# One-core hybrid decoder layer: more chunks multiplied with seven products instead of eight, in gate|up, down and the projections around the attentions

## The chip, the core and the metric

The kernel runs on one core of one Trainium2 chip. The metric is device time of one execution in microseconds (us). A core has a matrix engine (TensorE, PE in the profile; its weight loads are PEld), a vector engine (VectorE, DVE), a scalar engine (ScalarE, ACT), GpSimd (POOL) and SyncE (SP), which here only issues transfers. The engines run side by side and wait for each other by semaphores. VectorE and ScalarE take their instructions strictly in their own order; the program's order is fixed by hand for TensorE alone, and a scheduler orders the other engines.

## The reference, cut to what matters

256 tokens, model width 2048, float32 weights. One layer: half a SwiGLU, a mixing stage of a gated spatial MLP and a windowed attention, a cross-attention over 256 memory rows, another half SwiGLU, a final norm.

```python
def swiglu(x, w_gate, w_up, w_down):                  # w_gate, w_up 2048 x 5632, w_down 5632 x 2048
    return (jax.nn.silu(x @ w_gate) * (x @ w_up)) @ w_down

h = h + 0.5 * swiglu(rmsnorm(h, g_ffn1), w1_gate, w1_up, w1_down)
z = rmsnorm(h, g_mix) @ w_in                          # columns u | v | q | k | v'
y_a = spatial_gating(z[..., :o_q], g_v, w_s, b_s)
y_b = window_attention_sinks(z[..., o_q:o_k], z[..., o_k:o_v], z[..., o_v:], sinks)
h = h + concatenate([rmsnorm(y_a, g_a_out), rmsnorm(y_b, g_b_out)]) @ w_out
h = h + cross_attention(rmsnorm(h, g_x), rmsnorm(mem, g_mem), w_xq, w_xkv, w_xo)
h = h + 0.5 * swiglu(rmsnorm(h, g_ffn2), w2_gate, w2_up, w2_down)
return rmsnorm(h, g_final)
```

## The kernel before, in words

**Precision.** Every float32 operand is split into a high part (a cast on ScalarE, `split`, L150) and a low part (a subtraction on VectorE, L151). A float32 product is three matmuls: high by high, low by high, high by low.

**Chunks and units.** A weight chunk is 256 rows by 1024 columns, loaded as four blocks of 128 x 512 (B11, B12, B21, B22; `load`, L303). The 256 tokens are two blocks of 128, so the activations of a chunk are four blocks of 128 x 128 (A11, A12, A21, A22), held as a `Pair`. A unit (class `Unit`) accumulates a row of chunks (eight in most) in PSUM banks. A chunk of kind N or C takes eight block products, 24 matmuls; a chunk of kind S takes seven (a Strassen form), 21 matmuls, but needs sums of weight blocks (t, L314 to L318, with high and low parts th and tl) and sums of activation blocks. C is the eight-product form whose banks fit those of S (its pair holds S3 and S5), so a unit that has an S has no N beside it, apart from down and the output projections, which mix N and S. The strings `KINDS`, `KINDS_M`, `HALVES_O` and `KINDS_D` give the kinds of the chunks of a unit.

**After a unit.** When the last S is multiplied, `seven_early` takes P1, Q6 and Q7 out of their banks (one copy on ScalarE, two sums on VectorE). At the unit's end `seven_late` makes the four results with five sums on VectorE (L507 to L511).

**Stages in order.** Feed-forward 1: `plain_gu_unit` (unit 0 of gate|up, all N, fed by x as it is loaded), ten `gu_unit`s (L632, kinds `KINDS`), then down: 22 row chunks in three parts, four units over the parts (0), (0, 1), (1, 2), (2), each for one half of the columns (L665). Then the projections q, k|v, v, u from n2; memory values and keys (mv0, mv1, mk0, mk1); the output projection wo; xq from n3; the cross-attention; xo; feed-forward 2; the final norm and the stores.

**Order on TensorE.** `push` loads and splits a chunk and queues its multiplication; `turn` runs the queue one chunk late. Small work (transposes, attention, norms) sits in generators in `side`, and `side_step` puts one piece of it after every sixth matmul. `held`, `alone` and `tight` keep pieces out of some chunks. `seven_unit` (L513) first runs the side work until the attentions are done.

**Buffers.** Raw weights have three buffers, their high and low parts (wh, wl) two each, t, th and tl one each. Pairs come from `fp` (14 forms), small scratch from `tmp` (tag s2). PSUM has four banks for accumulators and four (`trp`) for P1, Q6, Q7 and all small work. In `attend` one such bank (`wop`, L933) collects the results of eight heads.

Of the kernel before, what the change touches and what calls it, by code (L numbers as in the profile page):

```python
# [8 lines left out]
F32 = mybir.dt.float32  # L9
# [11 lines left out]
WARM = 12  # L21
# [11 lines left out]
def layer_kernel(  # L33
# [29 lines left out]
    tmp = ctx.enter_context(tc.tile_pool(name="tmp", bufs=7))  # L63
# [21 lines left out]
    raw0 = s2("n0r").rearrange("p (k t) -> p k t", k=2)  # L85
    nc.scalar.dma_start(raw0, xT[:T, :].rearrange("(k p) t -> p k t", p=P))
# [36 lines left out]
    last_mean = [None]  # L123

    def rstd_of(parts, n, width, nt=TB):
# [7 lines left out]
        last_mean[0] = nc.vector.tensor_scalar(ms, ss, 1.0 / width, EPS, op0=ALU.mult, op1=ALU.add)  # L133
# [19 lines left out]
    def products(o, passes):  # L153
# [8 lines left out]

    BASE = {
        "N": ("A11", "A21", "A12", "A22"),
        "C": ("A11", "A12", "A21", "A22"),
        "S": ("A21", "A11", "A22", "A12"),
    }
    SUMS = {"N": (), "C": ("S3", "S5"), "S": ("S3", "S1", "S2", "S4")}
# [5 lines left out]
    class Pair:  # L174
        def __init__(self, s, kind, base=None):
            self.kind = kind
            self.base = base or form(s)
            if kind == "S":
                self.sums = form(s)
            elif kind == "C":  # L180
# [7 lines left out]
        def __getitem__(self, name):  # L188
            names, part = BASE[self.kind], self.base
            if name not in names:  # L190
                names, part = SUMS[self.kind], self.sums
            i = names.index(name)
            return part[0][:, i, :], part[1][:, i, :]

    def fill(s, p, raw):
# [5 lines left out]
        elif p.kind == "S":  # L201
# [4 lines left out]
        if p.kind == "S":  # L206
# [39 lines left out]
    def pair_loaded(s, raw, i, gcol, base):  # L246
        p = Pair(s, "N", base)
        for k in range(2):
            c = gcol + 2 * i + k
            hi, lo = [row_tile("N", t, k) for t in p.base]  # L250
            split_scaled(hi, lo, raw[:, k, :].rearrange("p (b t) -> p b t", b=2), sm[:, c:c + 1])
        return p
# [50 lines left out]
    def load(s, w, kind, pieces):  # L303
# [5 lines left out]
        if kind == "S":  # L309
            nc.sync.dma_start(raw, w)  # L310
            t = stream.tile([P, 4, 512], F32, tag="t", name=nm(s + "t"), bufs=1)
            th = stream.tile([P, 4, 512], F32R, tag="th", name=nm(s + "th"), bufs=1)
            tl = stream.tile([P, 4, 512], F32R, tag="tl", name=nm(s + "tl"), bufs=1)
# [6 lines left out]
            split(th, tl, t)  # L320
            for i, name in enumerate(("T1", "T3", "T2", "T4")):
                b[name] = th[:, i, :], tl[:, i, :]
        elif pieces:
            for i in pieces:
# [9 lines left out]
    class Unit:  # L334


        def __init__(self, s, kinds, late=("P1", "Q6", "Q7", "R"), alone=(), sparse=False):
# [10 lines left out]
            self.begun = set()  # L348
            self.banks = {}
# [4 lines left out]
        def multiply(self, kind, p, b, by_bank):  # L354

            steps, behind = [], []
            for name, *terms in PRODUCTS[kind]:
# [3 lines left out]
                for an, bn in terms:  # L361
                    (ah, al), (bh, bl) = p[an], b[bn]
# [3 lines left out]
            for n, (name, x, y) in enumerate(steps + behind):  # L366
# [7 lines left out]
            chunks_done[self.s] = chunks_done.get(self.s, 0) + 1  # L374
# [57 lines left out]
    def push(u, i, w, p, post=None, pieces=None, beside=None):  # L432
        b = load(u.s, w, u.kinds[i], pieces)
# [3 lines left out]
        def run():  # L437
# [5 lines left out]
            u.multiply(u.kinds[i], p(), b, i in (0, len(u.kinds) - 1))  # L443
# [6 lines left out]
    def unit(s, w, cb, pairs, late, beside=None):  # L450

        u = Unit(s, "N" * 8)
# [7 lines left out]
    def narrow_unit(s, w, pairs, late, beside):  # L460

        ps = []
        for c in range(2):
# [7 lines left out]
            def run(c=c, wh=wh, wl=wl):  # L471
                if c == 0:
                    ps.extend(acc.tile([P, 512], F32, tag="acc", name=nm(s)) for _ in range(TB))
                for k in range(8):
                    p = have(pairs, (c * 8 + k) // 2)
                    side_step()
                    for tb in range(TB):
                        hi, lo = p[f"A{tb + 1}{k % 2 + 1}"]
# [8 lines left out]
    KINDS = "CCSCSCSC"  # L487
    KINDS_M = "CCSCSCSC"

# [4 lines left out]
    KINDS_D = "NNNNSNSN" + "NNSNSNN" + "NNSNSNN"  # L494
# [18 lines left out]
    def seven_unit(s, w, cb, pairs, dst, late=None):  # L513

        u = Unit(s, KINDS_M, sparse=True)
        until(lambda: len(attended) == 2 * TB)
        got = {}

        def end():
            seven_late(u, got, dst)  # L520
# [3 lines left out]
        for i in range(8):  # L524
            push(
                u, i, w[i, cb], lambda i=i: have(pairs, i),
                (lambda: seven_early(u, got)) if i == 6 else end if i == 7 else None,
            )

    def adds(s, c, j0, on_block=None):  # L530
# [33 lines left out]
        def late(u):  # L564
            for name, tb, j in BLOCKS:
                add(hb(tb, j), u[name], tb, j)
                if on_block is not None:
                    on_block(j0 + j, tb)
# [15 lines left out]
    def ffn(s, get, rs, wgu, wd, on_block, first=None):  # L584
# [35 lines left out]
        def gu_unit(c):  # L620
# [11 lines left out]
            u = Unit(s + "g", KINDS)  # L632
            for i in range(8):
                push(
                    u, i, wgu[i, c], lambda i=i: get(i),
                    lambda i=i: seven_early(u, got) if i == 6 else late(u) if i == 7 else None,
                    beside=lambda i: (
                        rs() if (c, i) == (0, 5) else inner(i - 5) if c == 10 and i >= 5 else None
# [3 lines left out]
        def plain_gu_unit(c):  # L642
            pairs_, prep, rs0 = first
# [9 lines left out]
            for i in range(8):  # L653
                push(
                    u, i, wgu[i, c], lambda i=i: have(pairs_, i), late if i == 7 else None,
                    pieces=(1, 3, 0, 2) if c + i == 0 else None, beside=prep,
# [12 lines left out]
        for n, idx in enumerate(turns):  # L669
# [4 lines left out]
            for q, i in enumerate(idx):  # L674
                at += 1

                def ahead(q, at=at, kinds=kinds):
# [3 lines left out]
                    if kinds[q] == "N" and todo:  # L681
                        inner(todo[0])

                push(
                    u, q, wd[i, half], lambda i=i: (inner(i), pairs[i])[1],
                    lambda q=q, u=u, early=early, late=late, kinds=kinds:
                        early(u) if q == kinds.rindex("S") else late(u) if q == len(kinds) - 1 else None,
                    beside=ahead,
# [78 lines left out]
    ahead = [raw0]  # L767

    def prep1(i):
        if i % 2 == 0:  # L770
# [3 lines left out]
        raw = ahead.pop()  # L774
# [3 lines left out]
        if i == 2:  # L778
            blocks_of_x(2)
        n0.append(pair_loaded("n0", raw, i, G_FFN1, [t[:, i % 2] for t in quad]))  # L780
        if i == 1:
            blocks_of_x(0)
        for j in {3: (0, 1), 4: (2, 3)}.get(i, ()):
            for tb in range(TB):
                square_into(parts1[:, tb, j:j + 1], h[:, tb, j * 512:(j + 1) * 512], 512)
        if i == 4:
# [572 lines left out]
```

## Time and profile before

| | us |
|---|---|
| median of 3 runs | 2082.5 (2082.36 to 2082.59) |
| the profiled execution | 2082.59 |
| its span, first to last instruction | 2080.9 |
| PE busy | 2065.4 (99%) |
| DVE busy | 1684.6 (81%) |
| ACT busy | 1137.1 (55%) |

An engine is busy while one of its instructions runs; instructions that overlap are counted once in the tables by stretches, and each at its own length in the groups by line. The chain of work that ended last is followed back from the last instruction, at each step to what released it. A wait is put down to the instruction that came last.

### The profile page before, as it was taken

What the parts mean: (1) busy time and instruction counts of PE and PEld (TensorE: products, weight loads), DVE (VectorE), ACT (ScalarE), POOL (GpSimd) and SP (SyncE); (2) the same over time, 40 slices, a digit from 0 to 9 for tenths busy, and PEclk for the clock granted to TensorE, in tenths of its full rate; (3) what the DMA queues carried; (4) which work ended last, traced back from release to release, by engine and by line L of the source; (5) the groups of instructions that cost most, each with busy time, mean ns of one, the idle gap of its engine ahead of it and who ended that gap; (6) DMA issues with size and microseconds to landing.
All of it is one profiled execution on the core that took longest, in us unless ns stands there. A gap on an engine that the chain in (4) does not pass through costs nothing.

```text
span 2080.9 us, 23813 instructions
## 1 busy us (share of the span) xinstructions
PE 2065.4 (99%) x9518; PEld 1712.7 (82%) x9518; DVE 1684.6 (81%) x1621; ACT 1137.1 (55%) x1104; POOL 30.2 (1%) x51
## 2 busy tenths in 40 slices
PE   9999999999999999999999999999999999999998
PEld 7788888888888888888888888888888888888886
DVE  5988888888987845968888656798888888889877
ACT  7655555555544655555555455665555555555444
POOL 0000000000000000200000000000000000000000
PEclk9999999999999999999999999999999999999999
DMA  8555555555555564535555544455555555555563
GB/s 305 182 199 206 201 191 182 207 198 195 202 201 202 198 227 167 184 137 201 189 195 186 181 160 143 181 194 210 182 206 197 203 184 202 202 202 202 185 219 121
DMA packets 60111, 402.16 MB, mean 193 GB/s; under 512 B 6864, under 2 KB 8928, under 8 KB 12768
## 3 DMA queue, kind: packets, MB, share of 16 engines
q1 hardware_dynamic: 57280, 393.50, 52.7%
q0 software_dynamic: 2016, 6.30, 0.9%
q8 instruction: 74, 1.21, 0.2%
q10 hardware_dynamic: 704, 0.84, 0.1%
q14 instruction: 37, 0.30, 0.0%
HBM read 398.52 MB, written 2.10 MB: 193 GB/s over the span
## 4 chain that ended last, share of the span: by engine, by line
PE 97%; DVE 2%; ACT 1%; issue 0%; DMA 0%; POOLq 0%; POOL 0%; SPq 0%; DVEq 0%
PE f2gQ L368 16%; PE f1gQ L368 15%; PE f2dQ L368 6%; PE f1dQ L368 6%; PE f2gP L368 6%; PE f1gP L368 5%; PE f2dP L368 3%; PE f1dP L368 3%; PE woQ L368 2%; PE xoQ L368 2%; PE xqQ L368 2%; PE f2dR L368 2%; PE f1dR L368 2%; PE mk1Q L368 1%; PE mk0Q L368 1%; PE mv1Q L368 1%
## 5 line engine op out<-in xcount | busy, mean ns | idle before, releaser
L151 DVE TENSOR_TENSOR f1gwl<-f1gw,f1gwh 128x2048 fp32r<-128x2048 f32 (+1 forms) x91 | 185.7, 2042 | 55.8 <-ACT f1gwh L150 55.6
L150 ACT CAST f2gwh<-f2gw 128x1536 fp32r<-128x1536 f32 (+1 forms) x88 | 154.3, 1753 | 133.2 <-PE f2gQ L368 97.6
L150 ACT CAST f1gwh<-f1gw 128x2048 fp32r<-128x2048 f32 (+1 forms) x91 | 155.9, 1714 | 126.0 <-PE f1gQ L368 89.4
L151 DVE TENSOR_TENSOR f2gwl<-f2gw,f2gwh 128x1536 fp32r<-128x1536 f32 (+1 forms) x88 | 183.6, 2087 | 41.1 <-ACT f2gwh L150 40.9
L368 PE MATMUL f2gQ<-f2gwh,n4fh 128*128 128x512 f32 x363 | 141.4, 390 | 0.0
L368 PE MATMUL f2gQ<-f2gwh,n4fl 128*128 128x512 f32 x363 | 141.3, 389 | 0.0
L368 PE MATMUL f1gQ<-f1gwh,n1fh 128*128 128x512 f32 x330 | 128.8, 390 | 0.0
L368 PE MATMUL f1gQ<-f1gwh,n1fl 128*128 128x512 f32 x330 | 128.5, 389 | 0.0
L150 ACT CAST f1dwh<-f1dw 128x2048 fp32r<-128x2048 f32 (+1 forms) x44 | 79.1, 1797 | 84.5 <-PE f1dQ L368 65.3
L150 ACT CAST f2dwh<-f2dw 128x2048 fp32r<-128x2048 f32 (+1 forms) x44 | 79.1, 1797 | 83.3 <-PE f2dQ L368 67.8
L368 PE MATMUL f2gQ<-f2gwl,n4fh 128*128 128x512 f32 x363 | 115.7, 392 | 0.0
L151 DVE TENSOR_TENSOR f1dwl<-f1dw,f1dwh 128x2048 fp32r<-128x2048 f32 (+1 forms) x44 | 94.2, 2143 | 26.1 <-ACT f1dwh L150 23.5
L151 DVE TENSOR_TENSOR f2dwl<-f2dw,f2dwh 128x2048 fp32r<-128x2048 f32 (+1 forms) x44 | 94.2, 2143 | 22.8 <-ACT f2dwh L150 20.0
L368 PE MATMUL f1gQ<-f1gwl,n1fh 128*128 128x512 f32 x330 | 105.1, 392 | 0.0
L151 DVE TENSOR_TENSOR f2gtl<-f2gt,f2gth 128x2048 fp32r<-128x2048 f32 x33 | 75.6, 2291 | 17.9 <-ACT f2gth L150 17.4
L151 DVE TENSOR_TENSOR f1gtl<-f1gt,f1gth 128x2048 fp32r<-128x2048 f32 x30 | 68.7, 2291 | 16.7 <-ACT f1gth L150 16.2
L368 PEld LDWEIGHTS f2gQ<-f2gwh,n4fl 128*128 128x128 f32 x363 | 68.1, 188 | 14.2
L368 PEld LDWEIGHTS f2gQ<-f2gwh,n4fh 128*128 128x128 f32 x363 | 68.2, 188 | 14.1
L368 PEld LDWEIGHTS f2gQ<-f2gwl,n4fh 128*128 128x128 f32 x363 | 67.3, 188 | 13.5
L150 ACT CAST f2gth<-f2gt 128x2048 fp32r<-128x2048 f32 x33 | 63.1, 1912 | 24.8 <-DVE f2gt L318 20.0
L368 PEld LDWEIGHTS f1gQ<-f1gwh,n1fl 128*128 128x128 f32 x330 | 62.0, 188 | 12.8
L368 PEld LDWEIGHTS f1gQ<-f1gwh,n1fh 128*128 128x128 f32 x330 | 62.0, 188 | 12.8
(700 smaller groups left out, 5714.7 us busy)
## 6 DMA issues: line engine op xcount, KB each, us to landing
f2gw<-in_w_gu SPq DMA_DIRECT2D x88, 1024.0 KB, 4.8
f1gw<-in_w_gu SPq DMA_DIRECT2D x87, 1024.0 KB, 4.8
f1dw<-in_w_down SPq DMA_DIRECT2D x44, 1024.0 KB, 4.8
f2dw<-in_w_down SPq DMA_DIRECT2D x44, 1024.0 KB, 4.8
wow<-in_w_out SPq DMA_DIRECT2D x16, 1024.0 KB, 4.8
xqw<-in_w_xq SPq DMA_DIRECT2D x16, 1024.0 KB, 4.8
xow<-in_w_xo SPq DMA_DIRECT2D x16, 1024.0 KB, 4.8
qw<-in_w_in SPq DMA_DIRECT2D x8, 1024.0 KB, 4.9
```

Source lines behind the costliest of these rows:

```text
L150: nc.scalar.copy(hi, src)
L151: nc.vector.tensor_tensor(lo, src, hi.bitcast(F32), ALU.subtract)
L368: nc.tensor.matmul(self.banks[name], x, y, start=name not in self.begun, stop=self.left[name] == 0)
```

## The change

Chunks of kind S take the place of C or N: in units 2 to 9 of each gate|up (four of eight instead of three, and the S come first, `MORE`), in down (`KINDS_D`: parts 0 and 1 get one more S each), and in q, v and both xq units (two of eight each, where there was none; n2 and n3 are made with sums for that, as n4 was). Pair 0 of n1 and n4 gets a kind D, which holds both the sums of S and those of C, since units 1 and 10 use it as C. Before, `seven_early` ran at chunk 6; it still does in every unit, now found by the last S.

The tiles th and tl are cut in two halves (T1, T3 and T2, T4), each split by itself. In `attend` the results of each group of heads are copied out of a bank of their own. The wait for the attentions at the head of `seven_unit` is gone. The start loads x by rows ahead of the first weights and moves part of the preparation of n1 into unit 1. The last two chunks of feed-forward 2 are multiplied together, token block 0 first, and each block is finished (`finished`) as soon as it is complete. `tmp` has 6 buffers instead of 7, and 8 warming matmuls stand for 12.

```diff
-WARM = 12
+WARM = 8
-    tmp = ctx.enter_context(tc.tile_pool(name="tmp", bufs=7))
+    tmp = ctx.enter_context(tc.tile_pool(name="tmp", bufs=6))
-    nc.scalar.dma_start(raw0, xT[:T, :].rearrange("(k p) t -> p k t", p=P))
...
+        if p.kind == "D":
+            d = s2(s + "d")[:, :256].rearrange("p (k t) -> p k t", k=2)
+            nc.vector.tensor_tensor(d, raw[:, 1::2, :], raw[:, 0::2, :], ALU.subtract)
+            split(p.more[0], p.more[1], d)
...
-            split(th, tl, t)
+            for i, names in enumerate((("T1", "T3"), ("T2", "T4"))):
+                th, tl = [
+                    stream.tile([P, 2, 512], F32R, tag=f"{n}{i}", name=nm(s + n), bufs=1)
+                    for n in ("th", "tl")
+                ]
+                split(th, tl, t[:, 2 * i:2 * i + 2, :])
...
+        def multiply_two(self, first, second, between):
+            steps = [self.passes("N", p, b, True)[0] for p, b in (first, second)]
+            half = len(steps[0]) // 2
+            for tb in range(TB):
+                for k in range(tb * half, (tb + 1) * half, half // 2):
+                    for s in steps:
+                        self.run(s[k:k + half // 2])
+                between(tb)
...
-    KINDS = "CCSCSCSC"
+    KINDS = "DCSCSCSC"
+    FEWER, MORE = "CCSCSCSC", "SCSCSCSC"
     KINDS_M = "CCSCSCSC"
+    KINDS_MIX = "CCCSCCSC"
+    KINDS_X = "CCCSCCSC"
-    KINDS_D = "NNNNSNSN" + "NNSNSNN" + "NNSNSNN"
+    KINDS_D = "NNSNSNSN" + "NSNSNSN" + "NNSNSNN"
...
-        until(lambda: len(attended) == 2 * TB)
...
-            u = Unit(s + "g", KINDS)
+            u = Unit(s + "g", MORE if 2 <= c <= 9 else FEWER)
...
+                if on_token_block is not None and n == 3 and q >= len(kinds) - 2:
+                    def ending(tb, u=u, late=late):
+                        with tc.high_priority():
+                            late(u, (tb,))
+                            on_token_block(tb)
...
-        for j in {5: (0,), 6: (1,), 7: (2, 3)}.get(i, ()):
+        for j in {6:(0,),8:(1,),10:(2,),12:(3,)}.get(i, ()):
             normalized(j)
...
-    unit("q", w_in, 2, n2, late_q, beside_queries)
+    seven_unit("q", KINDS_MIX, w_in, 2, n2, None, late_q, beside_queries)
...
-            po = bank("wop")
+                po = bank("wop")[:, :per * 64].rearrange("p (a d) -> p a d", a=per)
+                nc.scalar.copy(ybh[:, hs, :], po)
...
-    unit("v", w_in, 1, n2, late_v)
+    seven_unit("v", KINDS_MIX, w_in, 1, n2, None, late_v, alone=(7,))
-    unit("u", w_in, 0, n2, late_u, beside_u)
+    unit("u", w_in, 0, n2, late_u, beside_u, alone=(0,7))
...
-        unit(
-            "xq", w_xq, cb, n3, lambda ps, cb=cb: late_xq(cb, ps),
+        seven_unit(
+            "xq", KINDS_X, w_xq, cb, n3, None, lambda at, cb=cb: late_xq(cb, at),
```

## Rows read from the trace of the kernel before

**Rows 1.** The page: the busy totals, and the chain that ended last.

```profile
PE 2065.4 (99%) x9518; PEld 1712.7 (82%) x9518; DVE 1684.6 (81%) x1621; ACT 1137.1 (55%) x1104; POOL 30.2 (1%) x51
PE 97%; DVE 2%; ACT 1%; issue 0%; DMA 0%; POOLq 0%; POOL 0%; SPq 0%; DVEq 0%
```

**Rows 2.** Busy time by stretches: stretch, length, each engine, clock, DMA share, GB/s.

```profile
60.00:102.78 42.78, 42.13 (x191) 33.85 (x190) 38.94 (x43) 26.02 (x27) 0.00 (x0) 1.00 0.55 196
...
780.00:943.00 163.00, 163.00 (x807) 134.69 (x806) 115.73 (x184) 88.88 (x149) 13.85 (x19) 1.00 0.46 162
...
1165.00:1300.00 135.00, 134.10 (x694) 113.70 (x693) 82.68 (x84) 70.73 (x85) 0.69 (x1) 1.00 0.44 156
...
1836.00:2069.00 233.00, 233.00 (x1033) 193.02 (x1032) 200.98 (x191) 119.82 (x97) 0.00 (x0) 1.00 0.52 185
...
1457.85:1500.28 42.43, 42.43 (x192) 35.14 (x192) 36.36 (x31) 22.67 (x17) 0.00 (x0) 1.00 0.56 198
```

**Rows 3.** The chain in order of time: start, length, engine and matmul count.

```profile
124.81 3.40 PE f1gQ L368 x15
```

**Rows 4.** VectorE's groups by line and shape: count, busy us, mean ns, idle before.

```profile
L151 DVE TENSOR_TENSOR f2gwl<-f2gw,f2gwh 128x2048 fp32r<-128x2048 f32 x55 | 125.7, 2286 | 31.2 <-ACT f2gwh L150 31.1
L151 DVE TENSOR_TENSOR f2gtl<-f2gt,f2gth 128x2048 fp32r<-128x2048 f32 x33 | 75.6, 2291 | 17.9 <-ACT f2gth L150 17.4
...
L151 DVE TENSOR_TENSOR f2gwl<-f2gw,f2gwh 128x1536 fp32r<-128x1536 f32 x33 | 57.9, 1755 | 9.9 <-ACT f2gwh L150 9.8
...
L314 DVE TENSOR_TENSOR f2gt<-f2gw 128x1024 f32<-128x1024 f32 x33 | 40.3, 1221 | 0.6
...
L318 DVE TENSOR_TENSOR f2gt<-f2gt,f2gw 128x512 f32<-128x512 f32 x33 | 22.7, 688 | 0.7
...
L151 DVE TENSOR_TENSOR mkh<-mkT,mkh 128x1024 fp32r<-128x1024 f32 x4 | 4.9, 1220 | 0.5 <-ACT mkh L150 0.5
...
L202 DVE TENSOR_TENSOR f1af<-f1a 128x256 f32<-128x256 f32 x6 | 2.3, 417 | 0.0
```

**Rows 5.** VectorE in order of time, end of one gate|up unit: start, length, [idle before].

```profile
1484.40 2.29 DVE L151 TENSOR_TENSOR f2gtl<-f2gt,f2gth 128x2048 fp32r<-128x2048 f32 x1 [0.76 <-ACT f2gth L150]
1488.89 2.29 DVE L151 TENSOR_TENSOR f2gwl<-f2gw,f2gwh 128x2048 fp32r<-128x2048 f32 x1 [2.19 <-ACT f2gwh L150]
1492.52 2.29 DVE L151 TENSOR_TENSOR f2gwl<-f2gw,f2gwh 128x2048 fp32r<-128x2048 f32 x1 [1.33 <-ACT f2gwh L150]
1494.73 0.68 DVE L501 TENSOR_TENSOR f2gv<-f2gQ,f2gp 128x512 f32<-128x512 f32 x1
```

**Rows 6.** ScalarE's groups by line and shape: a cast of 1024 columns.

```profile
L150 ACT CAST mkh<-mkT 128x1024 fp32r<-128x1024 f32 x4 | 4.2, 1055 | 2.7 <-PE xs L155 2.7
```

**Rows 7.** TensorE's waits over the span: total us, times, longest.

```profile
PE xoP L368 <- ACT xofh L150: 0.7, 1, 0.7
PE f1gQ L368 <- DVE f1gtl L151: 0.6, 1, 0.6
```

**Rows 8.** The start in order of time, ScalarE and TensorE.

```profile
6.18 0.51 ACT L144 ACTIVATE n0h<-n0r,sm 128x256 fp32r<-128x256 f32 x1 [0.84 <-DMA n0r<-in_xT]
...
6.74 0.50 PE L368 MATMUL f1gP<-f1gwh,n0h 128*128 128x512 f32 x1 [0.41 <-ACT n0h L144]
...
9.51 0.63 PE L368 MATMUL f1gP<-f1gwl,n0h 128*128 128x512 f32 x1
...
9.94 0.63 PE L368 MATMUL f1gQ<-f1gwh,n0h 128*128 128x512 f32 x1
...
15.38 0.39 PE L368 MATMUL f1gP<-f1gwh,n0h 128*128 128x512 f32 x1
```

**Rows 9.** The end in order of time: last sum, last power, last store issued.

```profile
2070.61 0.69 DVE L537 SCALAR_TENSOR_TENSOR h<-f2dQ,h 128x512 f32<-128x512 f32 x1
...
2073.36 0.93 POOL L135 TENSOR_TENSOR rs<-ms,mhalf 128x1 f32<-128x1 f32 x1 [0.92 <-DVE ms L133]
...
2075.53 0.48 SPq L1283 DMA_DIRECT2D out<-hg  x1
```

More of the change, by code (lines that the diff above doesn't have):

```diff
@@ L177, in __init__ @@
             self.base = base or form(s)
-            if kind == "S":
+            if kind in "SD":
                 self.sums = form(s)
+                if kind == "D":
+                    self.more = [
+                        const.tile([P, 2, P], F32R, tag="more" + t, name=nm(s + "more")) for t in "hl"
+                    ]
             elif kind == "C":
@@ L191, in __getitem__ @@
                 names, part = SUMS[self.kind], self.sums
+                if kind == "C" and self.kind == "D":
+                    names, part = SUMS["C"], self.more
             i = names.index(name)
@@ L301, in layer_kernel, with load @@
     }
-    def load(s, w, kind, pieces):
+    def load(s, w, kind, pieces, between):
         raw = stream.tile([P, 4, 512], F32, tag="raw", name=nm(s + "w"), bufs=3)
@@ L365, in multiply, with run @@
                     last.append((name, ah, bl))
-            for n, (name, x, y) in enumerate(steps + behind):
+            return steps, behind
+        def run(self, steps):
+            for n, (name, x, y) in enumerate(steps):
                 self.left[name] -= 1
@@ L430, in turn, with push @@
         later[:] = [(n - 1, f) for n, f in later if n]
-    def push(u, i, w, p, post=None, pieces=None, beside=None):
-        b = load(u.s, w, u.kinds[i], pieces)
+    def push(u, i, w, p, post=None, pieces=None, beside=None, before=None, ending=None):
+        if before is not None and i:
+            before(i)
+        b = load(u.s, w, u.kinds[i], pieces, lambda n: before(i, n) if i == 0 else None)
         if beside is not None:
@@ L448, in layer_kernel, with unit @@
     BLOCKS = (("P2", 0, 0), ("Q3", 0, 1), ("R", 1, 1), ("Q4", 1, 0))
-    def unit(s, w, cb, pairs, late, beside=None):
-        u = Unit(s, "N" * 8)
+    def unit(s, w, cb, pairs, late, beside=None, alone=()):
+        u = Unit(s, "N" * 8, alone=alone)
         for i in range(8):
@@ L526, in seven_unit @@
                 u, i, w[i, cb], lambda i=i: have(pairs, i),
-                (lambda: seven_early(u, got)) if i == 6 else end if i == 7 else None,
+                lambda i=i: (i == kinds.rindex("S") and seven_early(u, got), i == 7 and end()),
+                beside=beside,
             )
@@ L635, in gu_unit @@
                     u, i, wgu[i, c], lambda i=i: get(i),
-                    lambda i=i: seven_early(u, got) if i == 6 else late(u) if i == 7 else None,
+                    lambda i=i: (
+                        i == u.kinds.rindex("S") and seven_early(u, got), i == 7 and late(u)
+                    ),
                     beside=lambda i: (
-                        rs() if (c, i) == (0, 5) else inner(i - 5) if c == 10 and i >= 5 else None
+                        first[2](8 + i) if first is not None and c == 1
+                        else rs() if (c, i) == (0, 5) else inner(i - 5) if c == 10 and i >= 5 else None
                     ),
@@ L642, in plain_gu_unit @@
         def plain_gu_unit(c):
-            pairs_, prep, rs0 = first
+            pairs_, before, prep, rs0 = first
             u = Unit(s + "g", "N" * 8, alone=(7,))
@@ L766, in layer_kernel, with first_pairs @@
     quad = []
-    ahead = [raw0]
-    def prep1(i):
-        if i % 2 == 0:
+    ahead = []
+    def first_pairs(i, piece=None):
+        if i % 2 == 0 and not piece:
             quad[:] = [
@@ L773, in prep1 @@
             ]
-        raw = ahead.pop()
+        if not piece:
+            n0.append(Pair("n0", "N", [t[:, i % 2] for t in quad]))
+            if piece is not None:
+                ahead.append(s2("n0r").rearrange("p (k t) -> p k t", k=2))
+        for k in range(2) if piece is None else (piece,) if piece < 2 else ():
+            if piece is not None:
+                nc.sync.dma_start(ahead[0][:, k, :], xT[k * P:(k + 1) * P, :])
+            row_loaded(n0[i], ahead[0], i, k, G_FFN1)
+        if piece in (None, 1):
+            ahead.pop()
+    def prep1(i):
         if i < 7:
@@ L1254, in layer_kernel @@
     hg = [[m4("hg") for _ in range(2)] for _ in range(TB)]
+    known = [tiny.tile([P, 1], F32, tag="known", name=nm("known")) for _ in range(TB)]
+    summed = [[] for _ in range(TB)]
     def on_final(j, tb):
-        square_into(partsf[tb][:, j:j + 1], h[:, tb, j * 512:(j + 1) * 512], 512)
+        part = partsf[tb][:, j:j + 1]
+        square_into(part, h[:, tb, j * 512:(j + 1) * 512], 512)
+        summed[tb].append(part)
+        if len(summed[tb]) == 2:
+            nc.vector.tensor_tensor(known[tb], *summed[tb], ALU.add)
+        elif len(summed[tb]) == 3:
+            nc.vector.tensor_tensor(known[tb], known[tb], part, ALU.add)
+            nc.vector.tensor_scalar(known[tb], known[tb], 1.0 / D, EPS, op0=ALU.mult, op1=ALU.add)
         if j < 2:
```

177 lines of the change are left out of this document (94 added, 83 removed).

## Prediction, made before the changed kernel was run

> **What bounds the kernel now.** I read the page's totals first. TensorE is busy for 99% of the span and the chain that ended last is 97% TensorE [rows 1]; VectorE, at 81%, is the only other engine near its end. Then the table by stretches [rows 2]: in a steady gate|up unit (the last row of the group, 1457.85 to 1500.28) TensorE is busy for all of 42.43 us, VectorE for 36.36, ScalarE for 22.67, and the transfers take 0.56 of the DMA engines. So a unit lasts as long as its matmuls. One matmul of 512 columns costs 0.2267 us, 3.40/15 [rows 3]; a unit of five eight-product chunks (24 matmuls) and three seven-product chunks (21) has 183 of them, 41.5 us, and the remaining 0.9 us are its transposes. A removed matmul therefore gives 0.2267 us as long as VectorE keeps up, and what VectorE has left is 42.43 - 36.36 = 6.1 us per unit. That is the question of the whole change: it takes matmuls from TensorE and pays with VectorE work.
>
> **Matmuls removed.** Each chunk that turns from eight products to seven loses 3. Gate|up: one more in each of units 2 to 9, in two feed-forwards, 16 chunks, 48 matmuls, 10.9 us. Down: `KINDS_D` gains one S in part 0 and one in part 1, each used twice, in two feed-forwards, 8 chunks, 24 matmuls, 5.4 us. q, v and the two xq units get two S each, 24 matmuls, 5.4 us. Sum: 96 matmuls, 21.8 us, if nothing else moves.
>
> **What VectorE pays in gate|up.** An eight-product chunk costs it one subtraction of 2.286 us; a seven-product chunk costs the sums t (1.221 + 0.688 + 0.688, L317 being like L318), the low part of 1536 columns (1.755) and that of t (2.291), 6.64 us in all [rows 4]. One chunk converted: +4.35 us. All four low parts of t are also cut in halves, and two of 1024 columns take 2 x 1.220 against 2.291 [rows 4], +0.15 each, 0.6 per unit. So a changed unit asks VectorE for 36.36 + 4.35 + 0.6 = 41.3 us, and TensorE for 42.43 - 0.68 = 41.75. Instructions that wait for nothing start some 0.08 us before the end of the one ahead (1492.52 + 2.29 = 94.81, and the next starts at 94.73 [rows 5]), so the real demand is nearer 41.0. VectorE keeps 0.4 to 0.8 us of idleness in a unit instead of 6.1.
>
> The halves deserve a word, since the same rows price them both ways: a cut costs 0.15 us of VectorE and lets the low part start after a cast of 1.055 [rows 6] instead of one of twice that width, in a place where VectorE stood 0.76 us for that cast (1484.40 [rows 5]). The Trainium skill (VectorE: DVE Perf Modes, The TRN2 errata) speaks against it: a fixed cost is paid by each instruction whatever its width, so one large tile pays once and halves pay twice. The rows agree (2.44 against 2.29); by the page's formula of 151 cycles over the width the cut costs about 0.16 us, an estimate, and the unit would be the same 41.3.
>
> Can VectorE be that full without TensorE waiting? The waits it has now come in the second half of a unit: 0.76, 2.19 and 1.33 us for ScalarE's casts [rows 5], which themselves wait for TensorE to give the weight buffers back. That is running ahead, not being late; the new work goes into that room. The hard place is the border of two units. A unit now begins with an S, in order by bank, so its low parts are due within 0.5 to 4 us of the border, and in the same stretch VectorE owes two sums (`seven_early`), five (`seven_late`), and the S itself, 2.6 + 1.76 + 2.44: 1.4 + 3.4 + 6.8 = 11.6 us, less 0.7 of overlapped starts, 10.9. From the last plain chunk's due time (5.0 before the border) to the last due time (3.9 after it) there are 8.9 us. So VectorE must reach that place some 2 us early, with t already summed. In the six chunks before it gains: a pair S+C costs 8.9 against 10.2 of matmuls, 1.3 us each. By hand the order just fits, with handovers to ScalarE in between that I can't place. Ends: no stall (0), and a unit that is no shorter than now plus 0.5 (1.2 us per unit, 19 us). I take 0.3 per unit, 16 x 0.3 = **4.8 us** given back, nearer to none since TensorE lost nothing in these units so far: its largest waits in the whole trace after the start are 0.6 and 0.7 us [rows 7].
>
> **Down.** The second down stage: 233.0 us, VectorE 201.0 [rows 2]. Added: 4 x 4.35, 16 cuts x 0.15, and two more pairs with sums, each at most three subtractions of 0.417 and one more low part as wide as L318, 0.69 [rows 4], 3.9 for both: 23.7, so 224.7 of 230.3. That is 98%, and in the first unit of the stage (three S of eight, the pairs still being made, the last gate|up unit's sums pending) I count 44 us of VectorE against 41.5 of matmuls. Cover is what it ran ahead. Ends 0 and 4 per stage; I take 1, **2 us** for both.
>
> **Around the attentions.** Conversions 8 x 4.5, four units' seven sums (4 x 4.8), and the pairs of n2 and n3 with sums (about 12): some 67 us of VectorE, most of it in stretches where it idles 47 of 163 and 52 of 135 us [rows 2]. It fits, cost 0. In `attend` twelve small evictions replace a bank held for eight heads; ScalarE is busy 89 of 163 there, cost 0, and 2 if a score's eviction queues behind them. After xq the rows pass VectorE (`seven_late`) before ScalarE scales them, about 0.7 us later than now, and TensorE already waits 0.7 us for the end of that chain, in xo [rows 7]: ends 0 and 2, I take **0.7**.
>
> **First two units.** x now comes in two row loads, the first ahead of the weights on SP's queue. Today the first scaled row waits for its load until 6.18, the first matmul is at 6.74, and the second chunk starts at 15.38, 8.6 us for 24 matmuls worth 5.4; the pace near 9.5 is 0.43 us, the 1.2 GHz level [rows 8]. Half the bytes, queued first instead of behind `sm`, should bring the row about when the first weight piece comes, some 1 us earlier; the weights are queued one issue (0.4 us) later. I take **-1.0**, ends -2.5 and +1.5 (four fewer warming matmuls leave TensorE idle before the first row). Against it, three quarters of the pairs n1 move from unit 0 into unit 1: 6 pairs of 1.5 to 2.4 us, 11.6 us, onto a unit whose own VectorE work is some 35, in 44 to 45 of TensorE with the transposes; today unit 1 shows 38.9 of 42.8 [rows 2]. That is 2 us over, partly covered by unit 0: ends 0 and 3, I take **+1.0**. The third sum form of pair 0 (D) is 0.8 us once, inside this.
>
> **The tail.** The last sum starts at 2070.61, the last power ends at 2073.36 + 0.93, the last store is issued at 2075.53 [rows 9], and the span ends at 2080.9. In the new order token block 0 is summed, scaled and stored while block 1 multiplies (half of the last two chunks, 5.4 us). Block 1's chain is the same sum, square, mean and power, without waiting behind block 0's: about 1 us less on VectorE and POOL, and half the bytes at the end. Against it, the last two chunks now need both weights together, the second one's a chunk earlier than today, up to 1 us. I take **-1.7**, ends -3 and 0. One scratch buffer fewer (`tmp`, 7 to 6) lies under all stages; cost 0, inside the stalls taken above.
>
> **Sum:** -21.8 + 4.8 + 2 + 0.7 - 1.0 + 1.0 - 1.7 = -16.0. On the profiled execution, 2080.9 of span and 1.7 around it, 2066.6; the median of the runs is 0.1 lower: **2066.5 us**.
>
> **Rivals.** (a) VectorE becomes the bound of both feed-forwards: changed units stay near 42.4 and down wins nothing. Then 10.9 + 5.4 are lost instead of 6.8: -6.5, 2076. For: 41.0 to 41.3 of 41.75 leaves no room for waits it can't help. Against: most of its present waits are running ahead. (b) Everything is hidden: -21.8 - 2.7 + 1 = 2059. For: no stall of TensorE in any unit now. (c) Slower: at each border the S-first chunk finds VectorE at its due time, not ahead, and TensorE stands the whole 2 us worked out above; 16 x 2 = 32 in place of 4.8 gives +11, 2094. It decides from the point at which VectorE comes to the last chunk's low part less than 2 us early. Against: the 3.5 us it waits just before that place today. (d) The stalls of (a) also lower TensorE's clock. The trace shows one such fall, near 9.5, after a broken start, and that first chunk lost 3.2 us in all, 8.6 - 5.4 [rows 8]; half of it, 1.6, once per changed unit in addition to (a) is 26 us: 2102. But the wait of 0.7 us in xo [rows 7] stands in a stretch whose granted clock is 1.00 [rows 2]. The Trainium skill (TensorE: Matmul & The Clock Gate, HAM oscillation) has this as its warning, idle gaps putting the array back to half rate again and again; here only the start bears it out.
>
> **How the numbers follow.** Chances: forecast 0.50 (2061 to 2072), (a) 0.28 (2072 to 2080), (b) 0.15, (c) 0.05, (d) 0.02. The range leaves out (c), (d), the last us of (a) and the lower third of (b): 2058 to 2079. A measurement of this kernel can tell about 0.2%, 4.2 us, from no change: faster takes the forecast, (b) and three quarters of (a), 0.86; same the rest of (a), 0.07; slower (c) and (d), 0.07.
>
> **What would show it.** Changed gate|up units of 41.8 to 42.1 us with VectorE at 97% or more, and TensorE's waits there short and for a low part; that row of the second down stage near 231; first matmul before 6; the last store issued about 4 us after the last matmul. Wrong if units stay above 42.4, if the waits sit on PSUM banks at the border, or if the granted clock falls below 1.00 inside them.

## The result, and the profile after

The changed kernel takes 2063.66 us (2063.09 to 2064.23) against 2082.43 us for the one before on the same chip: a ratio of 0.991, 95% interval 0.9898 to 0.9922, so 18.8 us or 0.9% faster. The forecast was 2066.5, range 2058 to 2079. The profiled execution took 2063.49 us, its span is 2061.7 against 2080.9, and all of the following accounts for these 19.2 us.

The page of the changed kernel: busy time of each engine, and the chain that ended last.

```profile
PE 2043.0 (99%) x9414; PEld 1690.3 (82%) x9414; DVE 1845.6 (90%) x1973; ACT 1220.6 (59%) x1341; POOL 36.0 (2%) x53
PE 97%; ACT 1%; DVE 1%; issue 0%; DMA 0%; SPq 0%; POOL 0%; POOLq 0%; DVEq 0%; ACTq 0%
```

Against [rows 1] TensorE is still the bound (99%), now for 22.4 us less, while VectorE went from 81% to 90% for 161 us more work. Table by stretches of the changed kernel (stretch, length, each engine, clock, DMA share, GB/s): a changed unit of either gate|up, unit 1 of the first, and the second down stage, to set beside [rows 2].

```profile
263.76:305.56 41.80, 41.80 (x190) 34.49 (x189) 39.96 (x38) 24.08 (x21) 0.00 (x0) 1.00 0.55 202
1531.65:1573.47 41.82, 41.82 (x189) 34.49 (x189) 40.11 (x39) 24.23 (x22) 0.00 (x0) 1.00 0.55 201
52.00:96.60 44.60, 43.70 (x208) 35.82 (x207) 43.66 (x55) 33.78 (x45) 0.00 (x0) 1.00 0.48 171
1823.50:2051.00 227.50, 227.50 (x1010) 188.35 (x1009) 215.85 (x231) 126.01 (x119) 0.00 (x0) 1.00 0.52 185
```

The changed unit is 41.8 us long, not 42.43, and TensorE is busy in all of it; VectorE has 40.0 to 40.1 (96%) where the forecast had 41.0 to 41.3. The clock is 1.00 in all four stretches. TensorE's waits over the changed kernel's span (total us, times, longest), the lines of [rows 7]:

```profile
PE xoQ L400 <- ACT n4r L248: 2.5, 1, 2.5
PE f1gP L400 <- ACT f1gwh L146: 2.2, 2, 1.3
PE woQ L400 <- ACT n3r L248: 1.5, 1, 1.5
...
PE f1gQ L400 <- DVE f1sg L658: 0.9, 1, 0.9
PE qTp L928 <- ACT qs L914: 0.7, 1, 0.7
PE xoP L400 <- ACT xofh L146: 0.7, 1, 0.7
```

There is no wait for a low part of t. The two largest past the start are new and lie where nothing was expected: in xo (2.5) and in wo (1.5). The stages, each from its first matmul on the bank of its name to the next one's, us:

| stage | before | after | difference |
|---|---|---|---|
| start, unit 0 of the first gate\|up | 55.4 | 54.0 | -1.4 |
| unit 1 | 45.9 | 46.5 | +0.6 |
| units 2 to 10 | 381.9 | 376.8 | -5.1 |
| first down | 235.1 | 231.3 | -3.8 |
| q, v, u, attention | 352.9 | 352.2 | -0.7 |
| wo | 91.7 | 93.1 | +1.4 |
| xq | 103.5 | 100.7 | -2.7 |
| xo | 102.8 | 105.7 | +2.9 |
| second gate\|up | 469.1 | 463.0 | -6.1 |
| second down, to the last sum | 232.4 | 229.7 | -2.7 |
| after the last sum | 10.3 | 8.7 | -1.6 |

### The profile page after: what moved, and what is told of

The parts are those of the page before. It is cut to its first block, busy times and chain, and to the rows that moved or that the text cites. A ratio compares the mean times of both kernels' runs of the same rounds, so it can differ in the third digit from the quotient of the medians.

```text
span 2061.7 us, 24483 instructions
## 1 busy us (share of the span) xinstructions
PE 2043.0 (99%) x9414; PEld 1690.3 (82%) x9414; DVE 1845.6 (90%) x1973; ACT 1220.6 (59%) x1341; POOL 36.0 (2%) x53
## 4 chain that ended last, share of the span: by engine, by line
PE 97%; ACT 1%; DVE 1%; issue 0%; DMA 0%; SPq 0%; POOL 0%; POOLq 0%; DVEq 0%; ACTq 0%
PE f2gQ L400 16%; PE f1gQ L400 15%; PE f1dQ L400 6%; PE f2dQ L400 6%; PE f2gP L400 6%; PE f1gP L400 6%; PE xqQ L400 3%; PE f1dP L400 3%; PE f2dP L400 3%; PE woQ L400 2%; PE xoQ L400 2%; PE f1dR L400 2%; PE f2dR L400 2%; PE vQ L400 2%; PE qQ L400 2%; PE mk1Q L400 1%
## 5 line engine op out<-in xcount | busy, mean ns | idle before, releaser
L146 ACT CAST f1gwh<-f1gw 128x1536 fp32r<-128x1536 f32 (+2 forms) x94 | 152.9, 1628 | 87.3 <-PE f1gQ L400 54.7
L147 DVE TENSOR_TENSOR f1gwl<-f1gw,f1gwh 128x1536 fp32r<-128x1536 f32 (+2 forms) x94 | 181.7, 1935 | 23.9 <-ACT f1gwh L146 23.8
L147 DVE TENSOR_TENSOR f2gwl<-f2gw,f2gwh 128x1536 fp32r<-128x1536 f32 (+1 forms) x88 | 179.3, 2037 | 11.0 <-ACT f2gwh L146 10.9
L400 PE MATMUL f2gQ<-f2gwh,n4fl 128*128 128x512 f32 x317 | 123.4, 389 | 0.0
L146 ACT CAST f2gth<-f2gt 128x1024 fp32r<-128x1024 f32 x82 | 84.8, 1049 | 52.3 <-DVE f2gt L323 42.0
L146 ACT CAST f1gth<-f1gt 128x1024 fp32r<-128x1024 f32 x76 | 78.8, 1050 | 57.4 <-DVE f1gt L323 44.1
L147 DVE TENSOR_TENSOR f2gtl<-f2gt,f2gth 128x1024 fp32r<-128x1024 f32 x82 | 99.5, 1218 | 10.1 <-ACT f2gth L146 9.6
L147 DVE TENSOR_TENSOR f1gtl<-f1gt,f1gth 128x1024 fp32r<-128x1024 f32 x76 | 92.3, 1218 | 9.0 <-ACT f1gth L146 8.4
L400 PE MATMUL f2gQ<-f2gwl,n4fh 128*128 128x512 f32 x317 | 97.0, 390 | 0.0
L400 PE MATMUL f1gQ<-f1gwl,n1fh 128*128 128x512 f32 x286 | 87.1, 390 | 0.0
L400 PE MATMUL f2gP<-f2gwh,n4fh 128*128 128x512 f32 x176 | 69.5, 395 | 0.0
```

Source lines behind the costliest of these rows:

```text
L146: nc.scalar.copy(hi, src)
L147: nc.vector.tensor_tensor(lo, src, hi.bitcast(F32), ALU.subtract)
L400: nc.tensor.matmul(self.banks[name], x, y, start=name not in self.begun, stop=self.left[name] == 0)
```

## Experiments

All are edits of the changed kernel; "costs" means against its 2063.66 us, ratios are against the kernel before on the same chip, with 95% intervals. Two stretches differ between profiled executions without an edit there: the start (unit 0 ended between 52.8 and 55.0 us in the kernels that share it) and xo, where a fall of the clock adds 1.4 to 1.7 us in some (last section). So an edit is read from the stages that it touches, and the cost of the whole kernel stands beside it.

### The fourth seven-product chunk

```diff
-            u = Unit(s + "g", MORE if 2 <= c <= 9 else FEWER)
+            u = Unit(s + "g", FEWER)
```

> The changed kernel with the fourth seven-product chunk taken out of units 2 to 9 of both gate|up stages; all else stays. Theory (TensorE bounds these units and VectorE has room): 16 chunks give back 48 matmuls, about 0.63 us per unit as the two traces show (42.43 against 41.80), so 16 x 0.63 = 10 us longer, near 2073.7; VectorE in such a unit near 36.5 of 42.4. Rival (VectorE close to its bound, as forecast, 0.3 us per unit lost to it): only 6 us longer, near 2070.

Measured: 2074.92 us, ratio 0.9962 (0.995 to 0.9975). Each gate|up became 5.1 us longer (428.4, counted from unit 1, and 468.1), 0.64 us a unit: 10.2 of the 10.9 us that 48 matmuls are worth. So what the fourth chunk's VectorE work costs TensorE is about 0.05 us a unit, not the 0.3 of the forecast. (The whole kernel is 11.3 us longer; in its profiled execution 1.6 of that are the clock in xo.)

### Down with its old kinds

```diff
-    KINDS_D = "NNSNSNSN" + "NSNSNSN" + "NNSNSNN"
+    KINDS_D = "NNNNSNSN" + "NNSNSNN" + "NNSNSNN"
```

> The changed kernel with the kinds of the chunks of down as before. Theory (no stall in down): 24 matmuls of 0.2267 us return, 5.4 us longer, near 2069.1. Rival (the forecast's 1 us of stall in each down stage goes away with them): 3.4 us longer, near 2067.

Measured: 2068.38 us, ratio 0.9934 (0.9922 to 0.9947); 2.7 us more in each down stage (the first: 234.1, the second: 232.4), 5.5 in all, the whole worth of the 24 matmuls, 5.4. Nothing is given back there.

### The high and low parts of t in one piece

```diff
-            for i, names in enumerate((("T1", "T3"), ("T2", "T4"))):
...
+            th, tl = [
+                stream.tile([P, 4, 512], F32R, tag=n, name=nm(s + n), bufs=1) for n in ("th", "tl")
+            ]
+            split(th, tl, t)
+            for i, name in enumerate(("T1", "T3", "T2", "T4")):
+                b[name] = th[:, i, :], tl[:, i, :]
```

> The changed kernel with the high and low parts of t in one tile each, split whole, as before the change. Theory A (the halves are what lets a unit of four seven-product chunks run without waits: a whole tile is given back only after the last of its products, and its low part starts after a cast of 1.9 us instead of 1.05): TensorE waits for the low part of t, 0.3 to 1 us per changed unit and some in down, 5 to 20 us longer. Theory B (a fixed cost per instruction is all that the cut brings): VectorE gets 0.3 to 0.6 us per unit back, TensorE was not waiting, 0 to 1 us longer or shorter.

Measured: 2139.0 us, ratio 1.0269 (1.0255 to 1.0283): 75 us slower than with halves, and slower than the kernel before. The first gate|up took 455.8 us (+32.5), the second 490.4 (+27.4), the first down 239.0 (+7.6) and the second down 237.7 (+8.0). Units 2 to 9 are 3.6 us longer each. Theory A has the direction and the waits, but at most a quarter of the size. TensorE's waits in this kernel:

```profile
PE f1gQ L398 <- DVE f1gtl L147: 13.3, 9, 1.7
PE f2gQ L398 <- DVE f2gtl L147: 12.7, 8, 1.7
```

And VectorE in order of time (start, length, idle before), with the matmul at a unit's border and one of ScalarE's casts:

```profile
243.15 2.28 DVE L147 TENSOR_TENSOR f1gtl<-f1gt,f1gth 128x2048 fp32r<-128x2048 f32 x1
...
245.49 0.50 PE L398 MATMUL f1gQ<-f1gtl,n1fh 128*128 128x512 f32 x1 [1.65 <-DVE f1gtl L147]
...
261.75 0.69 DVE L323 TENSOR_TENSOR f1gt<-f1gt,f1gw 128x512 f32<-128x512 f32 x1
...
262.56 1.91 ACT L146 CAST f1gth<-f1gt 128x2048 fp32r<-128x2048 f32 x1 [3.87 <-DVE f1gt L323]
...
264.50 2.29 DVE L147 TENSOR_TENSOR f1gtl<-f1gt,f1gth 128x2048 fp32r<-128x2048 f32 x1 [2.06 <-ACT f1gth L146]
...
275.18 2.29 DVE L147 TENSOR_TENSOR f1gtl<-f1gt,f1gth 128x2048 fp32r<-128x2048 f32 x1 [2.05 <-ACT f1gth L146]
```

In the middle of the unit VectorE stands 2.06 us for the cast of the whole t. That cast had not waited for a buffer: ScalarE stood 3.87 us for VectorE's last sum of t (261.75 + 0.69), began 0.12 us after it and took 1.91 us, and only then could the subtraction start. The changed kernel at the same place of a unit, VectorE and ScalarE:

```profile
239.93 1.23 DVE L319 TENSOR_TENSOR f1gt<-f1gw 128x1024 f32<-128x1024 f32 x1
...
241.26 1.05 ACT L146 CAST f1gth<-f1gt 128x1024 fp32r<-128x1024 f32 x1 [0.66 <-DVE f1gt L319]
...
242.74 0.68 DVE L322 TENSOR_TENSOR f1gt<-f1gt,f1gw 128x512 f32<-128x512 f32 x1
...
244.48 0.68 DVE L323 TENSOR_TENSOR f1gt<-f1gt,f1gw 128x512 f32<-128x512 f32 x1
```

With halves the first one is cast before the last two sums of t are made, each cast is 1.05 us, and a unit has one wait of VectorE for such a cast, 1.19 us, in place of two of 2 us. (That the cast waited for TensorE to give th back, which theory A names as well, stands in the gate|up stages of this trace once: 6.7 us, in unit 2 of the first, where TensorE then lost 3.5.) The 4 us lost in each unit make VectorE late at the border, and TensorE waits 1.65 us there. This is rival (c) at the place that the prediction named, and with the smaller waits behind it at 3.6 us a unit where (c) had 2; the halves are what keeps it away. The 0.15 us that a cut costs is a tenth of what it saves at one such wait.

### A scratch buffer more, and the waits in xo and wo

```diff
-    tmp = ctx.enter_context(tc.tile_pool(name="tmp", bufs=6))
+    tmp = ctx.enter_context(tc.tile_pool(name="tmp", bufs=7))
```

(with some small tiles at one or two buffers, to make room)

> The changed kernel with 7 scratch buffers as before the change (the room comes from small statistics tiles that never had more than one or two owners). Theory (the two new waits of TensorE in wo and xo, 1.5 and 2.5 us for a bank whose transposed rows ScalarE had not yet copied out, come from the missing scratch buffer that this copy writes): both vanish, 4 us shorter, near 2059.7. Rival (they come from ScalarE's order, which has the weight casts ahead of that copy, with more work than before in the pairs): unchanged within 1 us.

Measured: 2064.93 us, ratio 0.9915 (0.9901 to 0.9928), and the same two waits, 2.5 and 1.5 us. The scratch buffer isn't their cause. What is, the changed kernel's order of time shows (ScalarE, then TensorE):

```profile
1334.10 1.47 ACT L146 CAST xowh<-xow 128x1536 fp32r<-128x1536 f32 x1
...
1335.47 1.04 ACT L146 CAST xoth<-xot 128x1024 fp32r<-128x1024 f32 x1
...
1336.42 0.83 ACT L248 ACTIVATE n4r<-n,sm 128x256 f32<-128x256 f32 x2
...
1337.30 0.50 PE L400 MATMUL xoQ<-xoth,xofh 128*128 128x512 f32 x1 [2.54 <-ACT n4r L248]
```

Rows of n4 have been transposed into a PSUM bank; the copy out of it is queued on ScalarE behind two casts of weights, 1.47 and 1.04 us, and the next matmul needs a bank. ScalarE is the fullest engine there, 95% against VectorE's 89% (the changed kernel, then the one before at about the same place):

```profile
1320.00:1337.00 17.00, 14.75 (x73) 11.90 (x71) 15.13 (x21) 16.23 (x25) 1.42 (x3) 1.00 0.71 261
```

```profile
1334.00:1351.00 17.00, 17.00 (x84) 14.11 (x83) 15.41 (x22) 15.41 (x23) 0.00 (x0) 1.00 0.63 228
```

Before, ScalarE had 15.41 us of the 17, and TensorE no wait. Around the wait in wo ScalarE has 13.35 us of 14, and had 8.64 before.

### When the pairs of the next norm are made

```diff
-            yield 4 if i % 2 == 0 and mixed else 1
+            yield (8 if i % 2 == 0 else 3) if mixed else 1
```

> The changed kernel with the pairs of n2, n3 and n4 made further apart (a pause of 8 and 3 steps in place of 4 and 1 ahead of each pair's transposes). Theory (the waits in wo, 1.5 us, and xo, 2.5 us, come from ScalarE, busy 95% of the 17 us around them with weight casts and these pairs in one queue): both waits shrink or vanish, with the fall of the granted clock that follows the longer one in some executions (1.7 us), 3 to 6 us shorter, near 2059. Rival (the work only collides with the next seven-product chunk): unchanged within 1 us, the waits at another place.

Measured: 2063.13 us, ratio 0.9908 (0.9893 to 0.9923). As the rival had it, the waits in wo and xo are gone (wo -1.8, xo -2.8 us), and the same amount came back elsewhere: xq +1.7, q +1.1, second gate|up +1.6, with new waits of 1.4 us on a weight cast of xq and 0.8 on rows of n2. For n4 alone (6 and 2 in place of 4 and 1):

> The changed kernel with the pairs of n4 alone made further apart (pauses of 6 and 2 steps in place of 4 and 1). Theory (in the run that did so for n2, n3 and n4 the xo stage gained 2.8 us, but the next stages lost as much, since later pairs met other casts; half the delay keeps the gain): the wait of 2.5 us in xo and the fall of the clock behind it go, and unit 0 of the second gate|up loses less than 0.5: 2 to 4 us shorter, near 2060.5. Rival (the wait only moves, ScalarE being full there): within 1 us of the changed kernel.

Measured: 2062.95 us, ratio 0.9907 (0.9894 to 0.9921). Again the rival: xo fell by 1.4 us, the second gate|up grew by 1.7, and its largest wait is the moved one:

```profile
PE f2gQ L400 <- ACT n4r L248: 1.7, 1, 1.7
```

In both runs a later due time didn't remove the waits, it moved them. Neither version can be told apart from the changed kernel.

### The fourth chunk in all eleven units

```diff
-            u = Unit(s + "g", MORE if 2 <= c <= 9 else FEWER)
+            u = Unit(s + "g", MORE)
```

> The changed kernel with four of eight seven-product chunks in every gate|up unit that is not plain: units 1 and 10 of the first, 0, 1 and 10 of the second feed-forward as well. Theory (VectorE has 1.7 us to spare in a steady unit and 3 us in unit 10): 5 x 0.63 = 3.1 us shorter, near 2060.5. Rival (unit 1 of the first feed-forward, with the pairs of n1, and units 10, with the first pairs of down, have no room): 0 to 3 us longer.

Measured: 2070.29 us, ratio 0.9942 (0.993 to 0.9955). The first gate|up is 3.5 us longer, the second 5.2, where 15 matmuls fewer should have given 3.4 us (waits for f1gtl 2.0, n4r 2.0, f2gtl 1.7 us). By units: in the first, unit 1 lost 1.1 us, the unit behind it 1.9 and unit 10 0.5; in the second, unit 0 lost 4.8 and unit 1 1.1, and unit 10 alone gave its 0.6. So the units in which pairs are made, and the ones behind them, have no room; the largest loss, in unit 0 of the second feed-forward, neither theory nor rival named.

### How much room a changed unit has

Two runs added subtractions of 256 columns to units 2 to 9 whose result nobody reads, four and eight a unit.

```diff
+    spare = const.tile([P, 256], F32, name="spare")
...
+                if 2 <= c <= 9 and i % 2 == 0:
+                    nc.vector.tensor_tensor(spare, band, band, ALU.subtract)
```

> The changed kernel with four more VectorE subtractions of 256 columns in each of units 2 to 9 of both gate|up stages (their result is read by nobody). Each takes 0.42 us, 0.34 from start to start, 1.4 us per unit, where VectorE idled 1.7 of 41.8. Theory (the room left is real): TensorE still bounds the units, at most 0.2 us per unit longer, 0 to 3 us in all, near 2065. Rival (a unit needs part of that idleness, since VectorE has to be early at the border of two units): 0.7 us or more per unit, 11 us or more in all.

> The same with eight such subtractions per unit, 2.7 us of VectorE where 1.7 were idle. Theory: VectorE becomes the bound, 1.0 us per unit beyond the room, 16 us longer in all, near 2080, with TensorE's waits in the units. Rival (the border decides earlier, and each wait there starts others): 2 us or more per unit, 32 us or more.

Measured: 2070.98 (ratio 0.995, 0.9937 to 0.9962) and 2078.34 us (0.9983, 0.9974 to 0.9992). Neither answers the question: these instructions wait for nothing, and they ran early instead of in their units. The tile's line of the first (shortest/median/longest ns, first to last start):

```profile
L685 DVE TENSOR_TENSOR spare<-band x64: 413/424/427, 12.6 to 181.2; 128x256 f32<-128x256 f32 x64
```

With eight they ran from 12.5 to 490.2 us. They slowed the first gate|up (429.1 and 436.2 us from unit 1 on; with four above all unit 1, with eight units 3 to 9 as well, some 1.3 us each) and left the second at 463.1. The next two runs tied each one to the low part just made, so that it can't run ahead:

```diff
+        if extra[0]:
+            low = wl[:, 1, :256].bitcast(F32)
+            nc.vector.tensor_tensor(spare, low, low, ALU.subtract)
...
+                extra[0] = 2 <= c <= 9 and i % 2 == 0
```

> In the run with four more subtractions per unit these went to the front of the kernel, since they waited for nothing. Here each reads the low part just made of its own chunk, so it stays in its unit: four in each of units 2 to 9 of both gate|up stages, one for each seven-product chunk, 1.4 us of VectorE per unit where 1.7 of 41.8 were idle (their result is read by nobody). Theory (the idle time is room): 0 to 0.2 us per unit, 0 to 3 us longer than the changed kernel, near 2065. Rival (VectorE has to be early at the border of two units, so that part of its idleness is needed): 0.7 us per unit or more, 11 us or more.

> The same with eight, one per chunk, 2.7 us of VectorE per unit. Theory: VectorE is the bound from 1.7 us on, 1.0 us per unit, 16 us longer, near 2080, VectorE idle under 0.3 us in such a unit. Rival (the waits at the border bring others with them, as with the whole t): 2 us per unit or more, 32 us.

Measured: 2070.08 us with four (ratio 0.994, 0.9927 to 0.9952) and 2093.16 with eight (1.0052, 1.0039 to 1.0064, slower than before). One costs VectorE 0.34 us (0.42 long, started about 0.08 under the end of the one ahead), so four are 1.36 us a unit and eight 2.72. The two gate|up grew by 2.9 and 3.2 us, 0.38 a unit; with eight by 15.7 and 13.4, 1.8 a unit. That is between theory and rival both times. Of both additions about 0.95 us was free, and from there on it costs close to one for one, though VectorE is never full. The stretch of about a unit with four, then with eight:

```profile
200.00:242.00 42.00, 41.93 (x189) 34.37 (x188) 40.94 (x42) 23.90 (x21) 0.00 (x0) 1.00 0.56 198
```

```profile
200.00:243.00 43.00, 41.72 (x185) 33.68 (x185) 41.08 (x44) 23.44 (x20) 0.00 (x0) 1.00 0.53 193
```

VectorE still idles 1.1 us with four and 1.9 with eight, while TensorE waits. Where it waits, the lines with eight say: for the first low parts of a unit, at the border, 6 or 7 times in each feed-forward:

```profile
PE f1gQ L406 <- DVE f1gtl L147: 4.1, 7, 0.6
PE f2gQ L406 <- DVE f2gtl L147: 3.9, 6, 0.7
PE f1gP L406 <- DVE f1gwl L147: 3.5, 7, 0.6
```

### The projections as plain units

q, v and xq again with eight products everywhere, and the pairs of n2 and n3 without sums:

```diff
-    seven_unit("q", KINDS_MIX, w_in, 2, n2, None, late_q, beside_queries)
+    unit("q", w_in, 2, n2, late_q, beside_queries)
...
```

> The changed kernel with q, v and xq in eight products only and n2 and n3 without sums, as before the change. Theory (the 24 matmuls are worth 5.4 us, and the new waits of 1.5 us in wo and 0.7 at q's transposes are the price of the pairs with sums): 5.4 - 2.2 = 3.2 us longer, near 2066.9, with both waits gone and the one in xo still there. Rival (no price, as forecast): 5.4 us longer, near 2069.

Measured: 2069.7 us, ratio 0.9939 (0.9925 to 0.9952), 6.0 us more. By the stages that it touches 5.4: first down +1.0 (a stage is counted to q's first matmul), q to attention +1.6, wo +0.1, xq +2.7. That is the rival, no price: these 24 matmuls do bring their 5.4 us. The wait of 2.5 us in xo stands without them, so it belongs to what the change does besides. In wo the wait of 1.5 us went and one of 0.7 for mk came, but the stage is as long as in the changed kernel, 93.1 us, 1.4 over the one before.

## Why the forecast held, point by point

**Matmuls, -21.8: right.** Taken back in three parts, they cost 10.2, 5.5 and 5.4 us, 21.1 of 21.8; the pace of [rows 3] is the price.

**Gate|up, +4.8 given back: mis-sized.** It is 0.7 (10.9 - 10.2). The step that failed is VectorE's demand, 41.0 to 41.3: in the second feed-forward it is 40.11, 3.75 more than [rows 2], where the sum had 4.35 + 0.6. The terms were single durations, and as such they were right: the instructions of a unit, added up at their own lengths, are 37.65 us before and 42.5 after, +4.8. What was missed is how far they overlap. When VectorE has a queue, instructions start before the one ahead ends: in the order of time of the changed kernel, in xo,

```profile
1334.30 0.68 DVE L147 TENSOR_TENSOR n4fl<-n4f,n4fh 128x512 fp32r<-128x512 f32 x1
1334.90 0.68 DVE L147 TENSOR_TENSOR n4fl<-n4r,n4fh 128x512 fp32r<-128x512 f32 x1
1335.50 0.41 DVE L147 TENSOR_TENSOR n4fl<-n4f,n4fh 128x256 fp32r<-128x256 f32 x1
```

the first two rows are 0.68 long and the starts are 0.60 apart. The prediction saw the 0.08 us and took off 0.3 in all. But a changed unit has 37 instructions instead of 29, and 2 waits of 0.1 us or more instead of 7, and the overlap in it went from 1.3 us to 2.4: 1.1 us more, which with the 0.1 in the lengths is the whole way from 41.3 to 40.1. The border of two units was the right place: with 2.72 us more TensorE stands there, and with t in one piece 1.7 us at a time. The unit has some 0.95 us of room before that happens, so rival (a) was nearer than a TensorE that is busy all the time lets one think.

**The halves: the row was right, their meaning wasn't.** The prediction set 0.15 us per cut against one wait of 0.76 us [rows 5]. They are worth 75 us. The Trainium skill (VectorE: DVE Perf Modes, The TRN2 errata) was cited for one large tile that pays the fixed cost once; the run with whole tiles has that saving and loses 3.6 us a unit, so here the measurement decides against taking that rule by itself: in pieces, the first cast and subtraction start before the last sum is made.

**Down, +2: mis-sized, 0.** In the 230.3 us that match the row of before (1821.1 to 2051.4) VectorE has 218.65, 95%, where 224.7 (98%) was expected. The reason is the same: single lengths grew by 23.2 us (23.7 in the sum), their overlap by 5.5.

**Attentions, 0 and +0.7: the term that was too small, about +5.** The conversions bring 5.4, but q to xo, with the 1.0 us that first down gained beyond its own chunks, gained only 0.2 us in all: 4.2 us went to wo and xo, about 1 to q to attention. The step that failed is not the price of the conversions: that is 0, as forecast, since with plain projections q to attention, wo and xo are still 0.9, 1.4 and 2.9 us longer than before the change (xo without the fall of the clock). It is the 0, and 0.7 in xo, that the sum put at everything else that changed there. The prediction read VectorE's idle time and ScalarE's 89 of 163 us in a long stretch, and searched for the loss at the last head's chain. That wait is still 0.7 us, as in [rows 7]. Most of the loss, 4.0 us, is two waits in short stretches in which ScalarE is 95% busy and a bank of rows of n3 or n4 waits for it. Which part of the change tips ScalarE there (the third form of sums of the first pair, the cut casts, the order of the rows) wasn't tried for itself and stays open. One run bears on it: with t in one piece wo took 91.4 us, without its wait, and the longest wait in xo was 1.9 us. So the cut casts have a part in the wait in wo, as far as a kernel shows it in which other things ran late too.

**First two units, -1.0 and +1.0: right in kind.** The start of the changed kernel, beside [rows 8]:

```profile
5.81 0.50 PE L400 MATMUL f1gP<-f1gwh,n0h 128*128 128x512 f32 x1 [0.90 <-ACT f1gwh L146]
...
9.70 0.63 PE L400 MATMUL f1gQ<-f1gwh,n0h 128*128 128x512 f32 x1
...
14.99 0.39 PE L400 MATMUL f1gP<-f1gwh,n0h 128*128 128x512 f32 x1
```

The first matmul is at 5.81 (forecast: before 6), 0.9 us earlier; the slow stretch near 9.7 is still there, a matmul 0.63 us long, so chunk 2 wins only 0.4 us, and the stage 1.4. That is one execution: with the same start the other kernels ended unit 0 between 52.8 and 55.0 us, 2.5 to 0.4 earlier than the one before. Unit 1 lost 0.6 us, with VectorE busy for 43.66 of 44.6 and a wait of 0.9 us for the last gate product of unit 0 (f1sg).

**Tail, -1.7: right, -1.6.** Last sum, last power and last store issued, beside [rows 9]:

```profile
2053.03 0.68 DVE L584 SCALAR_TENSOR_TENSOR h<-f2dQ,h 128x512 f32<-128x512 f32 x1
...
2054.80 0.55 POOL L1354 TENSOR_TENSOR rs<-ms,mhalf 128x1 f32<-128x1 f32 x1 [2.72 <-DVE ms L1350]
...
2056.56 0.44 SPq L1367 DMA_DIRECT2D out<-hg  x1
```

From the last sum to the last store's issue it is 3.5 us, 4.9 before.

**Sum.** -21.8 + 0.7 + 0 + 5.2 - 1.4 + 0.6 - 1.6 is -18.3. The other 0.9 us came in the second gate|up (-6.1 where its share of 10.2 is 5.1), in its unit 0: 44.7 us before, with waits of 0.4 and 0.3 us for the high and low part of t, and 43.7 after, without them. With t in one piece that unit takes 44.6 again, so the halves bring this too. The forecast of -16.0 came close because errors went both ways, and that is luck: 6 us too much for VectorE's stalls, about 4.5 too little for what happens between q and xo. In the feed-forwards it went as in (b); (a), (c) and (d) did not come, and (c) is what the kernel with t in one piece does.

## What to carry to other kernels

Price a nearly full engine by the distance of its starts in a stretch where it has a queue, not by single durations, and then look for its room at the place with the nearest due times, since the engine that idled 1.8 us of 42 here had half of that to give. Before an engine is given more work, look at the others in short stretches (here 17 us) at the points where stages overlap; a wait there was not cured by moving the work that shows up in it. Where a tile goes from one engine to another and back, cut it where its first part is ready earlier: the fixed cost of a cut, 0.15 us here, can be far less than the wait for the whole. And added work that is to measure room must depend on what it stands beside, or it runs elsewhere.

## What the runs showed of the chip that was not expected

After the same wait of TensorE in xo, 2.5 us, the granted clock fell in some executions and not in others. The stretch behind the wait in the kernel with seven scratch buffers, then the changed kernel's:

```profile
1340.00:1342.00 2.00, 2.00 (x6) 1.54 (x5) 2.00 (x4) 1.36 (x3) 0.00 (x0) 0.52 0.00 0
```

```profile
1340.00:1342.00 2.00, 2.00 (x11) 1.65 (x10) 2.00 (x4) 0.30 (x1) 0.00 (x0) 1.00 0.00 0
```

6 matmuls instead of 11 in 2 us, the 1.2 GHz level, and xo took 107.3 us instead of 105.7. In the profiled executions the fall stood behind this wait in eight kernels, and in the one with t in one piece behind a wait of 1.9 us at the same place. It did not in the changed kernel, nor in the one with the fourth chunk in all units (there it came behind a later wait of 1.8 us). It also came behind waits of 2.3 us (unit 1 of the first gate|up, both kernels with the untied additions) and 3.5 us (t in one piece). Past the first 15 us of the kernel it came behind no wait of up to 1.7 us; thirteen of those, of 1.65 to 1.73, stand in the two gate|up of the kernel with t in one piece. So one kernel can be 1.4 to 1.7 us apart from its like without its edit having caused it, and a difference of that size between two of these kernels can't be read as the edit's.
